# Hybrid encoder layer on one core: large element-wise passes of the DeltaNet phases taken off GpSimd

## The chip, the cores and the metric

One Trainium2 chip, one of its cores. The metric is the device time of one execution in microseconds (us); the time before is the median of three runs, 1222.3 us (1218.43 to 1222.52). Engines are named as the profile names them: PE is TensorE, PEld its weight loads, DVE VectorE, ACT ScalarE, POOL GpSimd, SP SyncE.

## What is computed

The reference is one encoder layer over two sequences of 512 and 256 tokens (768 in all, six tiles of 128), width 1024, in float32:

```python
h = rms_norm(x); proj = h @ w_in
att = window_attention(...)            # 8 query heads, 2 kv heads
dn = deltanet(...)                     # 4 heads of 128, both directions
x = x + rms_norm(concat([att, dn]) @ w_out)
x = x + rms_norm(cross_attention(rms_norm(x), mem, ...))   # 256 memory tokens
x = x + rms_norm(square(relu(rms_norm(x) @ w1)) @ w2)
```

The DeltaNet part needs, for each direction and head: a convolution over time of q, k and v; for each chunk a decay matrix `E`, a triangular matrix `L = -(k k') * E`, the inverse of `1 + L`, and the decayed attention product `(k q') * E`; then a scan over the chunks. The cross-attention needs keys and values of the normalised memory, `rms_norm(mem) @ xa_wkv`.

## The kernel before, in words

Float32 products are made on PE in a faster number format with a high and a low part: `hi` is the value rounded by ACT (line 107 for weights), `lo` the remainder `raw - hi` (line 108), and each product is three matmuls (hi hi, hi lo, lo hi). `Weights.emit` (line 93) does that for one unit of weights after another in a planned order: a transfer on SP's queue into one of two `raw` buffers (line 106), the copy on ACT (line 107), the subtraction on the engine that was passed in as `lo` (line 108). In the first half of the kernel that engine is GpSimd (lines 205 and 206); each kind of result tile, `whi` and `wlo`, has four buffers. From line 240 on (output projection, cross-attention, MLP) it is VectorE.

The order of work is that of `run` (line 192): projections and window attention; then `deltanet` for heads 0 and 1 while the convolution projections of heads 2 and 3 fill in (`proj_dn`, line 538); then `deltanet` for heads 2 and 3 while `fill` fills in (the z projections, the preparation of the memory, and its keys and values); then the output projection and the rest. `run(*gens)` only writes them one after the other. Which instruction really comes next on each engine is set at build time by a planner that takes program order as priority and its own costs for durations: DeltaNet's instructions stand first, and those of the later generators go where the planner sees an engine free. On the chip each engine then runs its own list strictly in that order.

`deltanet` has three parts. `prep` (line 676), for three groups of two tiles: two sets of four matmuls (lines 688 and 697), scaled out of PSUM by ACT into the single buffers `Gn` (line 693) and `Pa` (line 702); for each direction four DVE passes that form the exponent of the decay (line 708), its exponential on ACT (line 710), `L = Gn * E` on DVE (line 711) and `E = Pa * E` on GpSimd (line 712). `inverse` (line 714): DVE transposes (725, 726), a recurrence of 104 short DVE passes, `t = A * A` (line 734) and `A = A + t` (line 738), transposes again (741, 742), then small matmuls from line 764 on. The scan (`step`): matmuls with DVE, ACT and small GpSimd passes between them; each finished tile is normalised with two tiny GpSimd passes (883, 884) and a DVE pass (885).

`memory_prep` (line 368) takes four memory tiles of 128 x 1024: sum of squares on ACT (377), the scaling by the norm on GpSimd (379), eight transposes on PE into two PSUM banks (383), eight scaled copies out of PSUM on ACT (386), two rounded copies `hi` on ACT (388), and two subtractions `lo` on GpSimd (389).

Of the kernel before, what the change touches and what calls it, by code (L numbers as in the profile page):

```python
# [6 lines left out]
F32 = mybir.dt.float32  # L7
F32R = mybir.dt.float32r
AF = mybir.ActivationFunctionType
ALU = mybir.AluOpType  # L10
# [4 lines left out]
P = 128  # L15
# [42 lines left out]
def run(*gens):  # L58
    for _ in chain(*gens):
        pass  # L60
# [21 lines left out]
class Weights:  # L82
# [1 line left out]


    def __init__(self, nc, new, raw, lo):
        self.nc, self.new, self.raw, self.sub = nc, new, raw, lo.tensor_tensor
        self.q, self.done, self.n = [], {}, 0

    def plan(self, key, src, kk, n):  # L90
# [2 lines left out]
    def emit(self, upto):  # L93
        while self.n < min(upto, len(self.q)):
            key, src, kk, n = self.q[self.n]
            self.n += 1
            hi, lo = self.done[key] = self.new(kk, n)
            pool, size, bufs = self.raw
            rows = kk if callable(src) else size // n
            for k in range(0, kk, rows):  # L100
                c = slice(k, min(k + rows, kk))
                if callable(src):
                    raw = src()
                else:
                    raw = pool.tile([P, c.stop - k, n], F32, tag="raw", bufs=bufs, name="raw")
                    self.nc.sync.dma_start(raw, src[:, c])
                self.nc.scalar.activation(hi[:, c], raw, AF.Copy)  # L107
                self.sub(out=lo[:, c], in0=raw, in1=hi[:, c].bitcast(F32), op=ALU.subtract)  # L108

    def get(self, key, ahead=2):  # L110
        idx = next(i for i, u in enumerate(self.q) if u[0] == key)
# [4 lines left out]
class Kernel:  # L116
# [75 lines left out]
    def run(self):  # L192
        self.const, g_const = self.open("const")
        self.dram, g_dram = self.open("dram", space=DRAM)
        g_ps = self.banks(mm=2, tr=1, dnp=2, dns=1, wn=2)
        self.load_constants()
        self.scratch()


        big, g_big = self.open("big", side="left")  # L200
        self.hh, self.hl = (big.tile([P, 8, TOK], F32R, tag="big", bufs=2, name="h" + x) for x in "hl")
        cv, g_cv = self.open("conv", side="left")
        self.conv_buffers(cv)
        wp, g_w = self.open("wB", side="left")
        self.W = Weights(self.nc, lambda kk, n: [wp.tile([P, kk, n], F32R, tag=x, bufs=4, name="w" + x) for x in ("hi", "lo")],
                         (wp, 512, 2), self.nc.gpsimd)
        self.plan_b()
        self.plan_m()
        ap, g_ap = self.open("rope", side="left")
        k0, g_k0 = self.open("keep0", side="right")  # L210
        k1, g_k1 = self.open("keep1", side="right")
        pool, g = self.open("first", side="right")
        self.proj_first(pool, ap)
        self.close(g)
        at, g_at = self.open("att", side="right")
        keep0, keep1 = self.keep_tiles(k0), self.keep_tiles(k1)
        run(self.proj_att(ap, 1), self.proj_att(ap, 2))
        self.close(g_ap)
        run(merge((self.proj_dn(cv, 0, keep0, ("mm", "dnp")), 48), (self.window(at), 150)))
        self.close(g_at)  # L220
        dn, g_dn = self.open("dnw", side="right")
        self.dn_setup(dn)
        m0, g_m0 = self.open("mem0", side="right")
        run(self.deltanet(dn, 0, keep0), self.proj_dn(cv, 1, keep1, ("mm", "wn")))
        self.mem_gain = m0.tile([P, 8], F32, name="mgain")
        self.nc.sync.dma_start(self.mem_gain, self.a["mem_norm_g"][0].rearrange("(k p) -> p k", p=P))
        run(self.deltanet(dn, 1, keep1), self.fill(cv, m0, k0))

        group = []

        def unit(kk, n):

            if not group:
                i, unit.n = unit.n % 3 if unit.n < 6 else 0, unit.n + 1
                x = (big, big, wp)[i].tile([P, 2 if i == 2 else 3, 2, 1024], F32R, tag="big", bufs=1 if i == 2 else 2, name="w")
                group.extend((x[:, u, 0], x[:, u, 1]) for u in range(x.shape[1]))
            return [x.rearrange("p (k n) -> p k n", n=n) for x in group.pop(0)]

        unit.n = 0
        self.W = Weights(self.nc, unit, (wp, 512, 2), self.nc.vector)  # L240
        self.plan_c()
        self.W.emit(6)
        for g in (g_m0, g_dn, g_k1, g_k0, g_w, g_cv):
            self.close(g)
        self.close(g_ps)

        g_ps = self.banks(mm=3, tr=2, xa=2, up=1)
        self.hT = {}

        def h_tiles(s0, nt, side):  # L250
            pool, g = self.open(f"hx{s0}", side=side)
            self.hT[s0] = tuple(pool.tile([P, 8, nt * P], F32R, name=f"hx{s0}{n}") for n in "hl")
            return g

        g_h4 = h_tiles(*SEQS[1], "right")
        wp, g_w = self.open("wC", side="right")
        self.W.raw = wp, 1024, 2
        pool, g = self.open("tail", side="right")
        g_h0 = h_tiles(*SEQS[0], "left")
        up, g_up = self.open("up", side="left")  # L260
        xp, g_x = self.open("cross", side="left")
        self.tail(pool, xp)
        first = self.hidden(up)
        self.up(0, 4, first, "up", 0)
        for x in (g_x, g, g_w, g_ps):
            self.close(x)
        g_ps = self.banks(mm=4, y=4)
        wp, g_w = self.open("wD", side="right")
        self.W.raw, self.w2pool = (wp, 1024, 2), wp
        pool, g = self.open("mlp", side="left")  # L270
        self.mlp(pool, up, first)
        for x in (g, g_up, g_h0, g_w, g_h4, g_ps, g_big, g_dram, g_const):
            self.close(x)
# [94 lines left out]
    def memory_prep(self, m0, hh, hl):  # L368

        nc = self.nc  # L370
        for i in range(4):
            x = m0.tile([P, D], F32, tag="x", bufs=2, name="xm")
            src = self.a["mem_prompt"] if i < 2 else self.a["mem_sample"]
            nc.sync.dma_start(x, src[0, (i % 2) * P:(i % 2 + 1) * P, :])
            junk = m0.tile([P, D], mybir.dt.bfloat16, tag="junk", bufs=1, name="junk")
            ss = m0.tile([P, 1], F32, tag="ss", bufs=3, name="ss")
            nc.scalar.activation(junk, x, AF.Square, accum_out=ss)
            r = self.rsqrt(m0, ss, 1, 1.0 / D, EPS, "rs1")
            nc.gpsimd.tensor_scalar(x, x, r, 0.0, ALU.mult, ALU.add)
            for b in (0, 4):  # L380
                ps = self.ps(("tr", "mm")[b // 4], "tp")
                for j in range(4):
                    nc.tensor.transpose(ps[:, j * P:(j + 1) * P], x[:, (b + j) * P:(b + j + 1) * P], self.ident)
                h = x[:, b * P:(b + 4) * P].rearrange("p (k c) -> p k c", k=4)
                for j in range(4):
                    nc.scalar.activation(h[:, j], ps[:, j * P:(j + 1) * P], AF.Copy, scale=self.mem_gain[:, b + j:b + j + 1])
                hi, lo = hh[:, b:b + 4, i * P:(i + 1) * P], hl[b // 4][:, :, i * P:(i + 1) * P]
                nc.scalar.activation(hi, h, AF.Copy)
                nc.gpsimd.tensor_tensor(out=lo, in0=h, in1=hi.bitcast(F32), op=ALU.subtract)
            yield  # L390

    def memory_kv(self, pool, hh, hl):
# [283 lines left out]
    def prep(self, pool, half, keep, g, ts):  # L676

        nc = self.nc
        E, L = self.E[:, g], self.L[:, g]
# [19 lines left out]
        Pa = pool.tile([P, 4, P], F32, tag="S4", bufs=1, name="Pa")  # L699
# [3 lines left out]
        for d in range(2):  # L703
            ds = slice(4 * d, 4 * d + 4)
            for tt, t in enumerate(ts):
                for h in range(2):
                    e, col = 4 * d + 2 * tt + h, 4 * d + 2 * half + h
                    nc.vector.scalar_tensor_tensor(out=E[:, e], in0=E[:, e], scalar=self.cole[:, t, col:col + 1],
                                                   in1=self.emask[:, d], op0=ALU.subtract, op1=ALU.min)
            nc.scalar.activation(E[:, ds], E[:, ds], AF.Exp)  # L710
            nc.vector.tensor_tensor(out=L[:, ds], in0=Gn, in1=E[:, ds], op=ALU.mult)
            nc.gpsimd.tensor_tensor(out=E[:, ds], in0=Pa, in1=E[:, ds], op=ALU.mult)

    def inverse(self, pool):

# [606 lines left out]
```

## Time and profile before

| what | before |
|---|---|
| median of three runs | 1222.3 us |
| time of the profiled execution | 1220.31 us |
| its span | 1218.5 us |
| mean granted clock of PE | 0.965 |
| busy PE / DVE / ACT / POOL | 1117.1 / 706.6 / 530.5 / 438.7 us |

All times in the rows further down are from the start of the span. Busy time of PE counts a matmul at whatever clock was granted. The stretches that matter for the change are 227 to 300 us (`prep` and `inverse` of heads 0 and 1), 300 to 340 (their scan), 340 to 370 (`prep` of heads 2 and 3), 370 to 412 (their `inverse`), 412 to 470 (their scan) and 470 to 530 (the last values of the memory and the first tiles of the output projection).

### The profile page before, as it was taken

The page shows a single profiled execution, that of the slowest core. Times are in us where ns is not written, and L with a number is a line of the kernel's source. Part 1 is how long each engine was busy: PE and PEld are TensorE (multiplying, and loading weights), DVE is VectorE, ACT ScalarE, POOL GpSimd, SP SyncE. Part 2 cuts the span into 40 slices and gives each one's busy share as a digit, 9 for nine tenths or more (in the row PEclk, how much of TensorE's full clock was granted, in tenths as well). Part 3 has the DMA queues.
Part 4 walks back from the last instruction along what each step waited for, and adds up shares of the span by engine and source line. Part 5 has one row for each costly group of instructions (what it writes and reads, how often), then busy time and mean ns, then how long its engine had stood idle before and what let it go on. Part 6 is the DMA issues. An engine that isn't in the chain of part 4 may idle for free.

```text
span 1218.5 us, 17803 instructions
## 1 busy us (share of the span) xinstructions
PE 1117.1 (92%) x6800; PEld 955.7 (78%) x6800; DVE 706.6 (58%) x1183; ACT 530.5 (44%) x1123; POOL 438.7 (36%) x475
## 2 busy tenths in 40 slices
PE   5998999877987698889898989999999999999995
PEld 5887888766876586678787778888888888888884
DVE  5313564799569741446635646365658565658656
ACT  5336766664466333433534534432333323333322
POOL 5354321453147323011101137353526253527461
PEclk9999999988798899999999999999999999999998
DMA  6355321311123116842722142122212222212115
GB/s 198 97 173 162 96 62 26 90 42 44 28 70 109 45 48 203 268 135 87 236 76 70 70 138 84 55 70 70 87 52 69 70 70 69 87 52 61 45 52 172
DMA packets 108703, 113.81 MB, mean 93 GB/s; under 512 B 10079, under 2 KB 81867, under 8 KB 108619
## 3 DMA queue, kind: packets, MB, share of 16 engines
q1 hardware_dynamic: 100971, 99.55, 27.0%
q10 hardware_dynamic: 7648, 13.13, 2.9%
q8 instruction: 53, 0.87, 0.3%
q14 instruction: 31, 0.25, 0.1%
HBM read 91.27 MB, written 21.39 MB: 92 GB/s over the span
## 4 chain that ended last, share of the span: by engine, by line
PE 47%; DMA 4%; issue 3%; DVE 3%; POOL 3%; ACT 2%; ACTq 0%; POOLq 0%; DVEq 0%; SPq 0%
PE up L1194 7%; PE up L1195 7%; PE up L1196 7%; PE y L189 5%; PE y L187 5%; PE y L188 5%; DMA raw<-in_w_out 2%; PE mm L189 2%; PE mm L187 2%; PE mm L188 2%; POOL y L1256 1%; DVE w L108 1%; DMA raw<-in_xa_wo 1%; ACT w L107 1%; PE xa L1155 1%
## 5 line engine op out<-in xcount | busy, mean ns | idle before, releaser
L1199 POOL TENSOR_TENSOR hid<-hid 128x256 f32<-128x256 f32 (+1 forms) x64 | 61.1, 955 | 221.9 <-ACT hid L1198 213.1
L108 POOL TENSOR_TENSOR wlo<-raw,whi 128x512 fp32r<-128x512 f32 (+1 forms) x61 | 83.6, 1374 | 137.2 <-ACT whi L107 98.6
L189 PE MATMUL y<-w,hl 128*128 128x512 f32 x318 | 123.8, 389 | 0.5 <-DVE hl L183 0.5
L188 PE MATMUL y<-w,hh 128*128 128x512 f32 x318 | 123.7, 389 | 0.0
L187 PE MATMUL y<-w,hh 128*128 128x512 f32 x318 | 123.7, 389 | 0.0
L1238 DVE TENSOR_TENSOR y<-y,y 128x512 f32<-128x512 f32 x72 | 48.9, 683 | 107.1 <-PE y L189 107.1
L1198 ACT ACTIVATE hid<-up 128x256 f32<-128x256 f32 (+1 forms) x64 | 31.3, 488 | 177.2 <-PE up L1196 177.2
L1194 PE MATMUL up<-hx0h,w 128*128 128x512 f32 x256 | 100.0, 391 | 1.6 <-DVE hx0l L183 1.6
L108 DVE TENSOR_TENSOR w<-raw,w 128x1024 fp32r<-128x1024 f32 (+1 forms) x58 | 78.9, 1366 | 37.6 <-ACT w L107 37.6
L1195 PE MATMUL up<-hx0l,w 128*128 128x512 f32 x256 | 100.0, 390 | 0.0
L1196 PE MATMUL up<-hx0h,w 128*128 128x512 f32 x256 | 99.6, 389 | 0.0
L996 POOL TENSOR_TENSOR quad<-quad 128x1024 f32<-128x1024 f32 x28 | 77.4, 2764 | 33.2 <-DVE w L108 20.6
L108 DVE TENSOR_TENSOR w<-quad,w 128x1024 fp32r<-128x1024 f32 x49 | 72.6, 1492 | 12.5 <-ACT w L107 12.5
L1194 PE MATMUL up<-hx4h,w 128*128 128x256 f32 x256 | 72.2, 282 | 4.3 <-ACT hid L1198 4.3
L107 ACT ACTIVATE w<-raw 128x1024 fp32r<-128x1024 f32 (+1 forms) x58 | 55.5, 963 | 38.5 <-DMA raw<-in_w_out 14.1
L1195 PE MATMUL up<-hx4l,w 128*128 128x256 f32 x256 | 71.7, 280 | 0.1
L1196 PE MATMUL up<-hx4h,w 128*128 128x256 f32 x256 | 71.4, 279 | 0.0
L189 PEld LDWEIGHTS y<-w,hl 128*128 128x128 f32 x318 | 59.7, 188 | 13.3 <-DVE hl L183 0.9
L188 PEld LDWEIGHTS y<-w,hh 128*128 128x128 f32 x318 | 59.7, 188 | 12.4
L187 PEld LDWEIGHTS y<-w,hh 128*128 128x128 f32 x318 | 59.7, 188 | 12.4
L182 ACT ACTIVATE hh<-hid 128x768 fp32r<-128x768 f32 x37 | 31.4, 848 | 81.9 <-PE y L188 64.0
L107 ACT ACTIVATE whi<-raw 128x512 fp32r<-128x512 f32 (+1 forms) x61 | 37.9, 625 | 50.3 <-DMA raw<-in_xa_wkv 12.3
(373 smaller groups left out, 3152.4 us busy)
## 6 DMA issues: line engine op xcount, KB each, us to landing
raw<-in_mlp_w SPq DMA_DIRECT2D x36, 512.0 KB, 4.5
quad<-in_mlp_w SPq DMA_DIRECT2D x28, 512.0 KB, 4.6
raw<-in_w_in SPq DMA_DIRECT2D x44, 256.0 KB, 2.9
d_x<-x ACTq DMA_DIRECT2D x12, 512.0 KB, 2.6
x<-d_x SPq DMA_DIRECT2D x12, 512.0 KB, 3.8
x<-in_x_prompt SPq DMA_DIRECT2D x8, 512.0 KB, 3.7
raw<-in_xa_wkv SPq DMA_DIRECT2D x16, 256.0 KB, 2.9
d_att<-parts SPq DMA_DIRECT2D x12, 256.0 KB, 2.0
```

The source lines that it names most:

```text
L107: self.nc.scalar.activation(hi[:, c], raw, AF.Copy)
L108: self.sub(out=lo[:, c], in0=raw, in1=hi[:, c].bitcast(F32), op=ALU.subtract)
L182: nc.scalar.activation(hi, src, AF.Copy)
L187: nc.tensor.matmul(ps, lh, rh, start=first, stop=False)
L188: nc.tensor.matmul(ps, lh, rl, start=False, stop=False)
L189: nc.tensor.matmul(ps, ll, rh, start=False, stop=last)
L996: nc.gpsimd.tensor_tensor(out=out, in0=x, in1=y, op=ALU.subtract)
L1194: nc.tensor.matmul(ps, wh[:, k], hh[:, k], start=k == 0, stop=False)
L1195: nc.tensor.matmul(ps, wh[:, k], hl[:, k], start=False, stop=False)
L1196: nc.tensor.matmul(ps, wl[:, k], hh[:, k], start=False, stop=k == 7)
L1199: nc.gpsimd.tensor_tensor(out=r, in0=r, in1=r, op=ALU.mult)
L1238: nc.vector.tensor_tensor(out=y, in0=y, in1=ps, op=ALU.add)
```

## The change

Four moves. The low parts of weights: those of the attention projections, of the small gate projection and of DeltaNet's heads 0 and 1 stay on GpSimd; those of heads 2 and 3 (12 units), of z (8) and of the memory's keys and values (16) go to VectorE. The decayed attention product (line 712) goes to VectorE. The scaling of the memory by its norm (line 379) goes to ScalarE. The memory's high parts are rounded straight out of PSUM on ScalarE, which drops the eight copies of line 388, and its low parts are made by VectorE out of PSUM in 32 passes of 128 x 128 in place of GpSimd's eight of 128 x 512. All else is the same text.

```diff
-        self.nc, self.new, self.raw, self.sub = nc, new, raw, lo.tensor_tensor
+        self.nc, self.new, self.raw = nc, new, raw
+        self.sub = lambda key: lo(key).tensor_tensor
...
-                self.sub(out=lo[:, c], in0=raw, in1=hi[:, c].bitcast(F32), op=ALU.subtract)
+                self.sub(key)(out=lo[:, c], in0=raw, in1=hi[:, c].bitcast(F32), op=ALU.subtract)
...
-                         (wp, 512, 2), self.nc.gpsimd)
+                         (wp, 512, 2), lambda key: self.nc.gpsimd if key[0] in ("att", "ba") or key[0] == "dn" and key[2] < 2 else self.nc.vector)
...
-        self.W = Weights(self.nc, unit, (wp, 512, 2), self.nc.vector)
+        self.W = Weights(self.nc, unit, (wp, 512, 2), lambda key: self.nc.vector)
...
-            nc.gpsimd.tensor_scalar(x, x, r, 0.0, ALU.mult, ALU.add)
+            nc.scalar.activation(x, x, AF.Copy, scale=r)
...
-                h = x[:, b * P:(b + 4) * P].rearrange("p (k c) -> p k c", k=4)
+                hi, lo = hh[:, b:b + 4, i * P:(i + 1) * P], hl[b // 4][:, :, i * P:(i + 1) * P]
                 for j in range(4):
-                    nc.scalar.activation(h[:, j], ps[:, j * P:(j + 1) * P], AF.Copy, scale=self.mem_gain[:, b + j:b + j + 1])
-                hi, lo = hh[:, b:b + 4, i * P:(i + 1) * P], hl[b // 4][:, :, i * P:(i + 1) * P]
-                nc.scalar.activation(hi, h, AF.Copy)
-                nc.gpsimd.tensor_tensor(out=lo, in0=h, in1=hi.bitcast(F32), op=ALU.subtract)
+                    g = self.mem_gain[:, b + j:b + j + 1]
+                    nc.scalar.activation(hi[:, j], ps[:, j * P:(j + 1) * P], AF.Copy, scale=g)
+                    nc.vector.scalar_tensor_tensor(out=lo[:, j], in0=ps[:, j * P:(j + 1) * P], scalar=g,
+                                                   in1=hi[:, j].bitcast(F32), op0=ALU.mult, op1=ALU.subtract)
...
-            nc.gpsimd.tensor_tensor(out=E[:, ds], in0=Pa, in1=E[:, ds], op=ALU.mult)
+            nc.vector.tensor_tensor(out=E[:, ds], in0=Pa, in1=E[:, ds], op=ALU.mult)
```

## Rows read from the trace of the kernel before

**Rows 1.** Busy time of each engine, share of the span, instructions (the page's first part).

```profile
PE 1117.1 (92%) x6800; PEld 955.7 (78%) x6800; DVE 706.6 (58%) x1183; ACT 530.5 (44%) x1123; POOL 438.7 (36%) x475
```

**Rows 2.** Stretches: PE, PEld, DVE, ACT, POOL busy us; granted clock, DMA share, GB/s.

```profile
227.00:300.00 73.00, 57.56 (x396) 49.45 (x395) 70.96 (x169) 40.66 (x106) 33.69 (x28) 0.88 0.21 58
...
370.00:412.00 42.00, 24.30 (x135) 20.54 (x136) 41.24 (x113) 21.13 (x48) 22.69 (x20) 0.80 0.30 96
```

**Rows 3.** PE's waits from 150 to 560 us: total, times, longest.

```profile
PE tr L567 <- DVE room L562: 12.1, 2, 6.3
PE dnp L764 <- DVE C L741: 10.3, 1, 10.3
...
PE mm L504 <- ACT z L515: 6.3, 1, 6.3
PE dnp L688 <- ACT Gn L693: 2.4, 2, 2.2
...
PE dnp L697 <- ACT Pa L702: 2.1, 3, 1.0
```

**Rows 4.** Groups of POOL by form, 190 to 530 us: busy, mean ns, idle before.

```profile
L108 POOL TENSOR_TENSOR wlo<-raw,whi 128x512 fp32r<-128x512 f32 x35 | 48.7, 1392 | 104.9 <-ACT whi L107 77.0 <-PE tp L383 11.4 <-PE wS L936 6.0
L712 POOL TENSOR_TENSOR E<-Pa,E 128x512 f32<-128x512 f32 x12 | 17.4, 1465 | 12.4 <-ACT Pa L702 4.6 <-DVE L L711 4.1 <-DMA E<-d_gc 1.9
```

**Rows 5.** POOL's passes of line 108 alone, by stretch.

```profile
227.00:300.00 73.00, 17.61 (x11) 0.88 0.21 58
...
370.00:412.00 42.00, 7.84 (x6) 0.80 0.30 96
```

**Rows 6.** POOL's passes of line 389 alone, by stretch.

```profile
370.00:412.00 42.00, 8.00 (x6) 0.80 0.30 96
```

**Rows 7.** Groups of DVE by form, 190 to 530 us.

```profile
L824 DVE SCALAR_TENSOR_TENSOR C<-dns,negc,room 128x128 f32<-128x128 f32 x32 | 9.2, 344 | 9.8 <-PE dns L821 9.4 <-issue 0.3
L108 DVE TENSOR_TENSOR w<-raw,w 128x512 fp32r<-128x512 f32 x12 | 8.3, 692 | 18.8 <-ACT w L107 18.8
```

**Rows 8.** Lines 708 and 711 on their own: minimum/median/maximum ns, first and last start.

```profile
L708 DVE SCALAR_TENSOR_TENSOR E<-E,cole,emask x48: 337/346/1391, 227.2 to 358.4; 128x128 f32<-128x128 f32 x48
L711 DVE TENSOR_TENSOR L<-Gn,E x12: 675/682/1785, 230.6 to 369.6; 128x512 f32<-128x512 f32 x12
```

**Rows 9.** Groups of DVE by form, 227 to 247 us.

```profile
L708 DVE SCALAR_TENSOR_TENSOR E<-E,cole,emask 128x128 f32<-128x128 f32 x24 | 12.8, 600 | 5.4 <-DMA E<-d_gc 5.4
```

**Rows 10.** DVE's recurrence alone (lines 734, 738: passes on `t`), by stretch.

```profile
253.00:294.00 41.00, 26.13 (x104) 0.84 0.18 45
375.00:401.30 26.30, 25.72 (x54) 0.87 0.37 116
```

**Rows 11.** DVE in order of time in the second inverse: start, length of the merged piece.

```profile
390.46 2.67 DVE L734 TENSOR_TENSOR t<-A 128x136 f32<-128x136 f32 x2
393.06 0.47 DVE L738 TENSOR_TENSOR A<-A,t 128x136 f32<-128x136 f32 x2
```

**Rows 12.** Groups of ACT by form, 190 to 530 us.

```profile
L388 ACT ACTIVATE hm<-xm 128x512 fp32r<-128x512 f32 x8 | 5.0, 636 | 0.0
...
L377 ACT ACTIVATE junk<-xm 128x1024 bf16<-128x1024 f32 x2 | 2.1, 1050 | 0.0
```

**Rows 13.** The chain of waits, 440 to 560 us: start, length, piece.

```profile
466.40 1.30 POOL wlo L108
467.94 0.70 POOL oss L884
...
475.21 1.28 POOL wlo L108
```

**Rows 14.** ACT's waits from 227 to 300 us.

```profile
ACT whi L107 <- PE mm L505: 3.5, 1, 3.5
ACT whi L107 <- issue: 3.5, 2, 2.8
```

**Rows 15.** ACT's waits from 370 to 412 us.

```profile
ACT whi L107 <- DMA raw<-in_xa_wkv: 5.6, 1, 5.6
```

## The prediction

> **What bounds the kernel now.** I read the page's busy times first, then the stretches, then what PE waits for in them. PE is busy for 92% of the span [rows 1], so the time is PE's work plus the places where PE stands or runs at the lower clock. The stretches show where those are [rows 2]. From 227 to 300 us PE works 57.6 of 73 us and from 370 to 412 only 24.3 of 42, and in both DVE is the full engine (71.0 and 41.2 us). The granted clock in them is 0.88 and 0.80, a mix of 2.4 and 1.2 GHz, after PE had stood. So in these stretches DVE's list and the order of PE's list set the pace, not PE's work. PE's waits name the rest [rows 3]: 12.1 us in two waits for the convolution's last pass on DVE (line 562), 10.3 us in one for the end of the second inverse, 6.3 us for ACT's copy of z, and 4.5 us for `Gn` and `Pa` in `prep`. GpSimd itself is hardly named. Its passes matter in two other ways: DVE passes are longer while a large GpSimd pass runs, and ACT and the transfers wait for GpSimd's slow ends.
>
> **What GpSimd's passes cost DVE.** In the second inverse a pair of recurrence passes takes 0.47 us, and a like pair beside GpSimd's subtractions 2.67 us [rows 11]. Pairs follow each other every 0.39 us, so one pass alone is worth some 0.2 us. The first inverse's 104 passes took 26.1 us, that is 5.3 over 104 x 0.2; in the second, 54 passes took 25.7 us, and at some 0.24 for these, which hold the longest shapes, 13.0 would do: 12.7 over [rows 10]. Line 708's 24 passes in the first `prep` took 600 ns each [rows 9] against a least 337 [rows 8]: 24 x 0.263 = 6.3 us. So DVE can get back 6.3 + 5.3 = 11.6 us in the first stretch and 12.7 in the second inverse. As a rule this is in the Trainium skill, SBUF — State Buffer, section "SBUF: two separate sides": a GpSimd pass and a DVE pass with two SBUF inputs exclude each other, and the loser blocks fully. The trace agrees with the 2.67 beside the 0.47.
>
> **What DVE gets instead.** A low part costs GpSimd 1.39 us [rows 4] and DVE 0.69 [rows 7]. The decayed product costs 1.47 on GpSimd [rows 4]; on DVE the same shape with the same operands costs 0.68 undisturbed [rows 8]. In the first stretch stand 11 low parts [rows 5] and 6 of the 12 products: 11 x 0.69 + 6 x 0.68 = 11.7 us. In the second inverse stand 6 low parts [rows 5] and 6 of the memory's eight subtractions [rows 6]; these become 6 x 4 passes of 128 x 128 out of PSUM, and the nearest such pass (line 824) takes 0.344 [rows 7]: 6 x 0.69 + 24 x 0.344 = 12.4 us. So on DVE both stretches come out even: 11.6 returned for 11.7 added, 12.7 for 12.4. I count DVE's list in itself as **nothing**. Bounds: if none of the passes is placed inside the bound parts, it is 12 us less in each; if nothing is returned, 12 more in each.
>
> **What is left that shortens the time.**
> (a) `Pa` has one buffer, and PE and ACT wait for it while GpSimd takes 1.47 us per direction. At 0.68 a group of two directions is done 1.6 us sooner. Of the 4.5 us that PE waits for `Gn` and `Pa` I take 2 off.
> (b) PE's two waits of together 12.1 us for the convolution stay, as DVE's sum in that stretch stays: 0.
> (c) z. Its copies on ACT stand behind `prep`'s chain and behind two of the eight rounded copies of the memory, 0.64 us each [rows 12]. Those copies are gone: 1.3 us; with the shorter chain of (a) I take 3 of the 6.3 off. The norm scaling that ACT takes over (four passes of 128 x 1024, the nearest row 1.05 us [rows 12]) adds 4.2 us in place of 8 x 0.64 = 5.1, so ACT is not fuller.
> (d) The end of the second inverse. The last two of the memory's subtractions end shortly before 400 us and the first product with the memory's keys cannot start earlier; on PE's list the inverse's first matmul stands before it, and PE stands for 10.3 us. When the memory's low parts come from DVE right behind ACT's copy, these products can be placed before the inverse ends, and there are enough of them to fill the whole wait. That depends on the planner's order, which the trace cannot show: between 0 and 10.3, I take 5.
> (e) The tail. The chain that ends last passes three of GpSimd's low parts, 1.3 us each, between 466 and 477 us, and the small normalisation pass on GpSimd stands in line behind the first of them [rows 13]. With 0.69 each that is 3 x 0.6 = 1.8, and 1.2 for the pass that need not queue: 3 us. What is late next there is the transfer that the freed buffer starts, which then starts earlier too.
> Sum: 2 + 0 + 3 + 5 + 3 = 13 us. The profiled execution took 1220.3 us, 2.0 below the median of the runs shown; 1222.3 - 13 gives **1209 us**. Covers: GpSimd's remaining small passes are hidden by PE's work; the attention stretch before 227 us keeps its order but for the first two memory scalings, which ACT has room for. From 530 us on the instructions are the same.
>
> **The page's rule against this change.** Splitting a pass multiplies a fixed part: from the rows, 32 passes of 0.344 are 11.0 us where eight of 0.69 would be 5.5. The Trainium skill, VectorE: DVE Perf Modes, section on the TRN2 errata, says the same (a fixed cost per instruction, so tiles of 512 or more are wanted), and by its 120 + 128 cycles out of PSUM, an estimate, the 32 passes would be 8.3 us. By that the sum would be 2 us better in the second inverse; the row decides.
>
> **Rivals.**
> *DVE waits for weights (slower).* DVE runs its list in order. A low part on it waits for ACT's copy, and that waits for a raw transfer, 5.6 us inside the second inverse [rows 15], or for a buffer or ACT's own line, 3.5 and 3.5 us inside the first stretch [rows 14]. On GpSimd such waits cost nothing: it stood 104.9 us before line 108 [rows 4]. If the planner puts these low parts among the recurrence passes and takes the transfers for shorter than they are, DVE stands for 12.6 us in the stretches where it is the full engine; then each inverse ends later, (c) and (d) do not come, and (a) and (e) remain: 1222.3 + 12.6 - 5 = **1230 us**. It decides from the point where DVE's waits in its own list pass the 5 us of (a) and (e). For it: 71.0 of 73 us on DVE [rows 2], so nothing can be caught up. Against: the low parts come far down in program order, so the planner has reason to place them where DVE is free, after the inverses.
> *An even trade (no change).* DVE gives as it takes, and PE's order is as before: (c) and (d) stay. Then only (a) and (e) count: 1222.3 - 5 = **1217 us**.
> *The whole lock comes back (much faster).* GpSimd's large passes in the two stretches are 17.6 + 6 x 1.47 = 26.4 and 7.8 + 8.0 = 15.8 us. If DVE, or the passes behind it, had been held for all of that and not the 11.6 and 12.7 that I read, 18 us more are free, and with them the waits of 12.1, 10.3 and 6.3 go, beside (a) and (e): 12.1 + 10.3 + 6.3 + 5 = 34, **1188 us**. The rule of the Trainium skill named above, taken in full, would do that. Against: the measured excess is what it is.
>
> **How the numbers follow.** Forecast 0.50, even trade 0.20, DVE waits for weights 0.18, the whole lock 0.08, and 0.04 for a planner's order that moves something else, split evenly. About 0.5% (6.1 us) can be told from no change, so faster is below 1216.2 and slower above 1228.4. The forecast's own range, with (a), (c), (d) between nothing and their whole waits, is 1198 to 1217; a few of its cases and the even trade fall within 0.5%. Faster 0.60, same 0.22, slower 0.18. Signs differ, so the range reaches from **1190**, short of the whole lock, to **1229**, short of the full price of the waits.
>
> **What would show it.** Right: DVE's line 708 near 0.34 us and the second recurrence near 21 us in all; PE's wait at line 764 below 6 us; no wait for GpSimd's line 108 in the last chain; ACT's wait for line 712 gone. Wrong: DVE waiting for line 107's copy inside the two inverses, by more than 8 us together; or PE's waits at lines 567 and 764 as long as before, which would be the even trade.

## The result, and the profile after

The changed kernel took 1212.8 us (median of four runs, 1210.7 to 1215.1) where the kernel before took 1222.4: a ratio of 0.9941 with a 95% interval of 0.9916 to 0.9966. Measured a second time (the last experiment below) it was 0.9954 [0.9928, 0.998]. So it is faster by about half a per cent, and the forecast of 1209 is 3.8 us off. The profiled execution took 1215.1 us with a span of 1213.3, against a span of 1218.5 before. Lines up to 85 keep their numbers; behind that all lines of the new kernel are one higher, but for the rewritten lines of `memory_prep`, where 388 is ACT's rounded copy and 389 the low part on DVE.

The page's first part, busy time by engine. Beside [rows 1] POOL has 83 us less; DVE and ACT differ by less than 2 us, and PE has 2.9 us more for the same 6800 matmuls:

```profile
PE 1120.0 (92%) x6800; PEld 958.7 (79%) x6800; DVE 708.1 (58%) x1263; ACT 529.4 (44%) x1119; POOL 355.5 (29%) x415
```

The stretches, in the columns of [rows 2]:

```profile
227.00:300.00 73.00, 56.36 (x549) 47.59 (x548) 68.95 (x191) 43.01 (x108) 10.94 (x11) 0.88 0.19 47
...
353.00:366.00 13.00, 0.81 (x5) 0.81 (x5) 11.92 (x31) 11.34 (x27) 0.75 (x2) 0.63 0.08 20
...
400.00:410.00 10.00, 10.00 (x61) 7.68 (x60) 3.53 (x10) 2.53 (x8) 0.00 (x0) 0.50 0.01 2
410.00:420.00 10.00, 10.00 (x75) 9.21 (x73) 3.25 (x8) 2.23 (x6) 0.00 (x0) 0.61 0.09 26
```

DVE is still the full engine from 227 to 300 us. Two new things stand in the second half: from 353 to 366 us PE does almost nothing, and from 400 to 420 it works without a gap at a granted clock of 0.50 and 0.61, that is mostly at the lower of its two levels. In the kernel before, PE's work behind the end of the second inverse, from 412 to 480 us, had 0.97.

What PE waits for from 150 to 560 us, the answer to [rows 3]:

```profile
PE mm L505 <- DVE wlo L109: 15.2, 2, 8.5
PE tp L384 <- DVE hm L389: 12.2, 1, 12.2
PE tr L408 <- ACT kvo L402: 4.9, 2, 3.4
...
PE dnp L765 <- DVE C L742: 0.6, 1, 0.6
PE tr L568 <- ACT room L571: 0.5, 1, 0.5
PE mm L505 <- ACT z L516: 0.4, 1, 0.4
PE dnp L698 <- ACT Pa L703: 0.4, 1, 0.4
...
PE tr L568 <- DVE y L563: 0.4, 1, 0.4
```

Every wait of [rows 3] has nearly gone, and two others stand in their place. Both are for low parts on DVE: the weights' (`wlo`, line 109) and the memory's (`hm`, line 389). Over the whole span PE stands (span less busy time) 93.3 us where it stood 101.4. Of these 8.1 us its longer busy time takes 2.9 back, and the 5.2 us between the spans are left.

DVE's passes on `t`, by stretch, the answer to [rows 10]. Together they returned 6.6 and 14.1 us (the second recurrence took 33.4 us before: 25.72 for the 54 passes shown and 7.67 for the other 50):

```profile
250.00:284.00 34.00, 19.48 (x104) 0.81 0.15 39
...
361.00:386.00 25.00, 19.29 (x104) 0.82 0.25 82
```

Where the gain went shows in two marks. One is the start of DVE's last transpose of each inverse; the other is ACT's copy of the memory's values, the last of which ends the work that the second inverse holds up. First the kernel before (count, least/median/most ns, first and last start), then the kernel after:

```profile
L742 DVE STREAM_TRANSPOSE C<-A x2: 1204/1212/1221, 295.3 to 410.9; 128x1024 f32<-128x1024 f32 x2
...
L409 ACT ACTIVATE kvv<-tr x4: 581/598/600, 476.4 to 501.5; 128x512 f32<-128x512 f32 x4
```

```profile
L743 DVE STREAM_TRANSPOSE C<-A x2: 1203/1204/1204, 286.3 to 389.2; 128x1024 f32<-128x1024 f32 x2
...
L410 ACT ACTIVATE kvv<-tr x4: 579/597/599, 474.9 to 496.3; 128x512 f32<-128x512 f32 x4
```

The first inverse ends 9.0 us sooner and the second 21.7. At the last of the memory's values only 5.2 us are left, and 5.2 is also the difference of the spans. So the change is decided by about 500 us: it wins 21.7 us up to the end of the second inverse and gives 16.5 of them back before 497.

It gives them back at the memory's low parts. DVE's order of time around the start of the second inverse, and then PE's:

```profile
356.77 3.32 DVE L726 STREAM_TRANSPOSE C<-L 32x384 f32<-32x384 f32 x4
360.12 0.35 DVE L389 SCALAR_TENSOR_TENSOR hm<-tp,mgain,hm 128x128 fp32r<-128x128 f32 x1
360.39 1.24 DVE L727 STREAM_TRANSPOSE A<-C 128x1024 f32<-128x1024 f32 x1
361.55 0.31 DVE L389 SCALAR_TENSOR_TENSOR hmr<-tp,mgain,hm 128x128 fp32r<-128x128 f32 x1
...
363.96 0.35 DVE L389 SCALAR_TENSOR_TENSOR hm<-tp,mgain,hm 128x128 fp32r<-128x128 f32 x1 [0.41 <-ACT hm L388]
...
364.79 0.34 DVE L389 SCALAR_TENSOR_TENSOR hm<-tp,mgain,hm 128x128 fp32r<-128x128 f32 x1
```

```profile
351.79 1.16 PE L698 MATMUL dnp<-room 128*128 128x128 f32 x8
365.19 1.11 PE L384 MATMUL tp<-ident,xm 128*128 128x128 f32 x4 [12.25 <-DVE hm L389]
```

PE's next transposes of the memory need a PSUM bank that is free only when the fourth low part out of it has run. These passes stand on DVE's list behind `prep`'s passes, behind 3.3 and 1.2 us of transposes, and then between passes of the recurrence; the fourth starts at 364.8 and PE at 365.2. Before, ACT alone emptied these banks, and GpSimd subtracted out of SBUF. The last low parts run only at 411.8 and 415.8 us, long after the inverse:

```profile
L389 DVE SCALAR_TENSOR_TENSOR hmr<-tp,mgain,hm x16: 310/344/351, 347.7 to 411.8; 128x128 fp32r<-128x128 f32 x16
L389 DVE SCALAR_TENSOR_TENSOR hm<-tp,mgain,hm x16: 338/344/351, 360.1 to 415.8; 128x128 fp32r<-128x128 f32 x16
```

### The profile page after: what moved, and what is told of

The parts are those of the page before. It is cut to its first block, busy times and chain, and to the rows that moved or that the text cites. A ratio compares the mean times of both kernels' runs of the same rounds, so it can differ in the third digit from the quotient of the medians.

```text
span 1213.3 us, 17783 instructions
## 1 busy us (share of the span) xinstructions
PE 1120.0 (92%) x6800; PEld 958.7 (79%) x6800; DVE 708.1 (58%) x1263; ACT 529.4 (44%) x1119; POOL 355.5 (29%) x415
## 4 chain that ended last, share of the span: by engine, by line
PE 42%; issue 3%; POOL 2%; DVE 2%; DMA 1%; ACT 1%; POOLq 0%; DVEq 0%; ACTq 0%
PE up L1195 7%; PE up L1196 7%; PE up L1197 7%; PE y L189 5%; PE y L188 5%; PE y L190 5%; POOL y L1257 1%; DMA raw<-in_xa_wo 1%; PE xa L1156 1%; PE xa L1137 1%; PE mm L1121 1%; PE mm L1120 1%; PE mm L1119 1%; POOL rs L153 1%; PE mm L188 0%
## 5 line engine op out<-in xcount | busy, mean ns | idle before, releaser
L190 PEld LDWEIGHTS y<-w,hl 128*128 128x128 f32 x318 | 59.7, 188 | 13.3 <-DVE hl L184 0.9
L184 DVE TENSOR_TENSOR hl<-hid,hh 128x768 fp32r<-128x768 f32 x37 | 43.0, 1162 | 24.8 <-ACT hh L183 24.6
L1195 PEld LDWEIGHTS up<-hx0h,w 128*128 128x128 f32 x256 | 48.1, 188 | 10.4 <-DVE hx0l L184 1.2
```

Of the source, the lines that this page charges most:

```text
L184: nc.vector.tensor_tensor(out=lo, in0=src, in1=hi.bitcast(F32), op=ALU.subtract)
L190: nc.tensor.matmul(ps, ll, rh, start=False, stop=last)
L1195: nc.tensor.matmul(ps, wh[:, k], hh[:, k], start=k == 0, stop=False)
```

## The experiments

Three kernels make one part of the change alone, each on the kernel before. Then parts of the change are taken back or moved, GpSimd work is put in, and the memory's low parts are made in two other ways. All ratios are to the kernel before, run beside it on the same chip. There it took 1218.0 us beside the three single parts and the kernel with heads 2 and 3 back on GpSimd, 1219.3 beside the last two, and 1216.9 beside the others; absolute times are to be read against these. The planner orders the instructions of every kernel anew, so each edit is measured together with the order that it brings.

**The product alone.**

```diff
-            nc.gpsimd.tensor_tensor(out=E[:, ds], in0=Pa, in1=E[:, ds], op=ALU.mult)
+            nc.vector.tensor_tensor(out=E[:, ds], in0=Pa, in1=E[:, ds], op=ALU.mult)
```

> Before, with the decayed product (line 712) alone moved to VectorE. Theory A (GpSimd's large passes lengthen VectorE's two-input passes, and the change gives that time back): line 708's 24 passes in the first prep fall from 600 ns to under 400, that stretch ends some 4 us sooner, the second prep some 2; both recurrences stay as long as before (26 and 33 us). Time 1216 to 1220. Theory B (the passes do not disturb each other; only the planner's new order counts): line 708 stays near 600 ns, time 1222 within 2.

Measured: 0.9959 [0.9936, 0.9982], some 5 us, as expected. DVE's line 708 in the first `prep` falls from 600 ns [rows 9] to 382, but the recurrences, beside which no product runs, keep most of theirs, 24.9 and 32.8 us for 26.1 and 33.4. PE's waits from 150 to 560 us:

```profile
PE dnp L764 <- DVE C L741: 13.4, 1, 13.4
PE tr L567 <- DVE room L562: 11.1, 4, 6.0
```

So the product shortens `prep` and nothing else: the two large waits of before stay.

**The weights' low parts alone** (the selection by key, with the rest of `Weights` as in the change).

```diff
-                         (wp, 512, 2), self.nc.gpsimd)
+                         (wp, 512, 2), lambda key: self.nc.gpsimd if key[0] in ("att", "ba") or key[0] == "dn" and key[2] < 2 else self.nc.vector)
```

> Before, with the low parts of 36 weight units alone moved to VectorE. Theory A: the first recurrence falls from 26 to about 20 us, the second from 33 to about 26 (the memory's passes on GpSimd still stand beside it); TensorE waits for low parts in VectorE's list, some 10 to 15 us in the first stretch, so the sum is small: 1214 to 1222. Theory B: recurrences as before; time set by the order alone, 1222 or more.

Measured: 0.9896 [0.9853, 0.9939], 1203.2 us. By its median this part alone gains more than the whole change (the intervals overlap a little). It is also more than the 1214 to 1222 us expected of it from a before of 1222, of which the ratio makes 1210: the waits for low parts are 6.3 and 1.4 us, not 10 to 15. The recurrences take 19.5 and 25.2 us, and the last copy of the memory's values starts at 479.0 us, 17 us before that of the change. PE's waits:

```profile
PE tr L408 <- ACT kvo L402: 6.8, 2, 4.7
PE mm L190 <- DVE wlo L109: 6.3, 1, 6.3
PE tr L568 <- DVE room L563: 5.6, 1, 5.6
```

**The memory alone** (`memory_prep` as in the change).

```diff
-            nc.gpsimd.tensor_scalar(x, x, r, 0.0, ALU.mult, ALU.add)
+            nc.scalar.activation(x, x, AF.Copy, scale=r)
...
-                    nc.scalar.activation(h[:, j], ps[:, j * P:(j + 1) * P], AF.Copy, scale=self.mem_gain[:, b + j:b + j + 1])
...
-                nc.scalar.activation(hi, h, AF.Copy)
-                nc.gpsimd.tensor_tensor(out=lo, in0=h, in1=hi.bitcast(F32), op=ALU.subtract)
...
+                    nc.scalar.activation(hi[:, j], ps[:, j * P:(j + 1) * P], AF.Copy, scale=g)
+                    nc.vector.scalar_tensor_tensor(out=lo[:, j], in0=ps[:, j * P:(j + 1) * P], scalar=g,
+                                                   in1=hi[:, j].bitcast(F32), op0=ALU.mult, op1=ALU.subtract)
```

> Before, with the memory's scaling and high and low parts alone changed (ScalarE, VectorE). Theory A: the second recurrence falls from 33 to about 25 us, the first stays near 26; TensorE's transposes of the memory wait for VectorE's low parts to free the bank, 5 to 12 us, so about even: 1216 to 1224. Theory B: second recurrence stays at 33 us.

Measured: 1.0088 [1.0054, 1.0122], slower by about 11 us, although the second recurrence falls from 33.4 to 23.6 us. PE's waits:

```profile
PE tr L567 <- DVE room L562: 13.4, 2, 7.8
PE tp L383 <- DVE hm L388: 8.7, 1, 8.7
...
PE dns L829 <- DVE C L824: 5.7, 3, 4.7
```

The wait for the memory's bank is there with this part alone. These rows do not show the loss itself: of the six executions, 1218 to 1231 us, the profiled one is the shortest, PE stands in it 102.3 us against 101.4 before, and its mean granted clock is 0.969 where the other five had 0.959 to 0.964. The three parts make -0.41, -1.04 and +0.88%, together -0.57%; the change measured -0.59 and -0.46%. It is about their sum: two gains and a loss.

**The change without the memory's part** (`memory_prep` as before).

```diff
-            nc.scalar.activation(x, x, AF.Copy, scale=r)
+            nc.gpsimd.tensor_scalar(x, x, r, 0.0, ALU.mult, ALU.add)
...
+                    nc.scalar.activation(h[:, j], ps[:, j * P:(j + 1) * P], AF.Copy, scale=self.mem_gain[:, b + j:b + j + 1])
...
-                    nc.scalar.activation(hi[:, j], ps[:, j * P:(j + 1) * P], AF.Copy, scale=g)
-                    nc.vector.scalar_tensor_tensor(out=lo[:, j], in0=ps[:, j * P:(j + 1) * P], scalar=g,
-                                                   in1=hi[:, j].bitcast(F32), op0=ALU.mult, op1=ALU.subtract)
+                nc.scalar.activation(hi, h, AF.Copy)
+                nc.gpsimd.tensor_tensor(out=lo, in0=h, in1=hi.bitcast(F32), op=ALU.subtract)
```

> The changed kernel with the memory's preparation as before (scaling and low parts on GpSimd, eight rounded copies on ScalarE). If the parts add up (product -0.4%, weights -1.0%, memory +0.9% when done alone), this is about 0.986 of before, 1201 us where before is 1218. Theory: TensorE's 12.2 us wait for the memory's low parts at the bank goes; the second recurrence grows from 19.3 to about 25 us, as in the run with the weights alone. Rival (the parts overlap, the sum being set by VectorE's fullness in the inverses): between the weights alone and the change, 0.990 to 0.994.

Measured: 0.9896 [0.9867, 0.9925], 1203.7 us. The loss goes when the part is taken back. But it is no better than the weights alone, so the product's 0.4% does not show on top (both intervals are as wide as that). The added-up 0.986 lies just outside the interval and the rival's 0.990 inside it. The second recurrence takes 27.5 us. PE's waits, in which no bank of the memory stands for DVE:

```profile
PE mm L505 <- DVE wlo L109: 14.5, 3, 9.3
PE wn L505 <- DVE wlo L109: 5.6, 1, 5.6
```

**Heads 2 and 3 back on GpSimd.** The low parts of these heads' weights are those that PE waited 15.2 us for.

```diff
-... or key[0] == "dn" and key[2] < 2 else ...
+... or key[0] == "dn" else ...
```

> The changed kernel, with the 12 low parts of heads 2 and 3 back on GpSimd. Theory A with the cost side (TensorE's 15.2 us of waits for low parts in VectorE's list are what the change gives back): those waits fall under 3 us, the first recurrence grows from 19.5 to about 25 us, and the net is a gain of 5 or more on the changed kernel: 1203 to 1208. Rival (those waits stand where TensorE would wait for the convolution on VectorE anyway): no gain or a loss, 1212 to 1218.

Measured: 1.0000 [0.9977, 1.0023]. The waits for `wlo` are gone, and the ratio is worse than the change's. The recurrences stay short, 20.5 and 19.3 us; the 25 expected of GpSimd's passes beside the first did not come. In this order, though, at most four of GpSimd's low parts stand beside it, where seven stood in the kernel before. PE's waits:

```profile
PE dnp L765 <- DVE C L742: 8.8, 1, 8.8
PE tp L384 <- DVE hm L389: 7.8, 1, 7.8
PE tr L568 <- DVE room L563: 5.7, 2, 3.6
```

**The same low parts earlier on DVE** (the planner's high priority for them).

```diff
...
-                self.sub(key)(out=lo[:, c], in0=raw, in1=hi[:, c].bitcast(F32), op=ALU.subtract)
+                with self.soon(key):
+                    self.sub(key)(out=lo[:, c], in0=raw, in1=hi[:, c].bitcast(F32), op=ALU.subtract)
...
+        self.W.soon = lambda key: self.tc.high_priority() if key[0] == "dn" and key[2] > 1 else nullcontext()
...
```

> The changed kernel, with the low parts of heads 2 and 3 put ahead in the planner's priority, so that they stand on VectorE's list before the DeltaNet passes and not among the recurrence. Theory (TensorE's two waits of 15.2 us for these low parts are a cost of the order): the waits fall under 4 us, time 5 to 10 us below the changed kernel. Rival (TensorE waits in the same stretch for something else of VectorE's): waits for line 563's convolution pass or the inverse's end take their place, time within 3 us of the changed kernel.

Measured: 1.0007 [0.9988, 1.0025]. Again no wait for `wlo`, and again no gain. PE's waits (this kernel's lines are four higher behind the diff):

```profile
PE dnp L769 <- DVE C L746: 12.7, 1, 12.7
PE tp L388 <- DVE hm L393: 7.8, 1, 7.8
```

The inverses end at 293.3 and 400.7 us in place of 286.3 and 389.2. So in these two orders the 15.2 us are not won, by order or by engine: with the low parts sooner, PE waits at the inverse's end. What is short there is DVE's time.

**GpSimd's passes put back, needless ones.** Eight passes of 128 x 512 at the start of each recurrence, on a buffer that nothing reads before it is rewritten; the outputs do not use them.

```diff
         nc.vector.transpose(A, C1)
+        lk = C2[:, 0:16]
+        nc.gpsimd.tensor_tensor(out=lk, in0=C1[:, 0:16], in1=C1[:, 16:32], op=ALU.subtract)
+        for j in range(7):
+            nc.gpsimd.tensor_tensor(out=lk, in0=lk, in1=lk, op=ALU.subtract)
```

> The changed kernel with eight needless GpSimd passes of 128 x 512 (subtractions on a buffer that is free then) during each recurrence; their result is not used and the planner's order on the other engines is nearly the same. If GpSimd's passes hold up VectorE's two-input passes: each recurrence grows from 19.4 us by 6 to 10 us, the GpSimd passes themselves take more than 1.28 us each where they meet it, and the time grows by 5 to 15 us. If not: recurrences within 1 us, time within 3 us of the changed kernel.

Measured: 1.0069 [1.0051, 1.0087]. DVE's passes on `t`, by stretch; in the change they take 19.5 and 19.3 us:

```profile
220.00:320.00 100.00, 24.48 (x104) 0.86 0.19 52
320.00:440.00 120.00, 23.84 (x104) 0.84 0.18 54
```

The same 104 passes grow by 5.0 and 4.5 us, about 0.6 for each needless pass; 6 to 10 were expected. The cause that the prediction read out of the pairs of 2.67 and 0.47 us [rows 11] is thus shown, at a smaller size. By the ratios the kernel is some 14 us slower than the change; in its trace PE waits 15.4 us for a low part of the memory (line 389) alone. The planner's order of the other engines was not wholly the same, so only the recurrences are read from it, not the total.

**The memory's low parts out of SBUF, whole.** As the change, but ACT first copies the scaled memory to SBUF, where it rounds it and DVE subtracts in eight passes of 128 x 512.

```diff
...
+                    nc.scalar.activation(h[:, j], ps[:, j * P:(j + 1) * P], AF.Copy, scale=self.mem_gain[:, b + j:b + j + 1])
...
-                    nc.scalar.activation(hi[:, j], ps[:, j * P:(j + 1) * P], AF.Copy, scale=g)
-                    nc.vector.scalar_tensor_tensor(out=lo[:, j], in0=ps[:, j * P:(j + 1) * P], scalar=g,
-                                                   in1=hi[:, j].bitcast(F32), op0=ALU.mult, op1=ALU.subtract)
+                nc.scalar.activation(hi, h, AF.Copy)
+                nc.vector.tensor_tensor(out=lo, in0=h, in1=hi.bitcast(F32), op=ALU.subtract)
```

> The changed kernel with the memory's low parts on VectorE, but as eight passes of 128 x 512 out of SBUF (the scaled copy is written to SBUF on ScalarE first, as before, and its eight rounded copies are back), so the PSUM bank is free after ScalarE's copies. If the bank held for VectorE is the memory part's cost: TensorE's 12.2 us wait goes, and the time is near that of the kernel with the memory as before, within 3 us. If VectorE's fullness is: time near the changed kernel.

Measured: 0.9818 [0.98, 0.9837], 1194.4 us, by clear intervals below the change and below the kernel with the memory as before; neither theory expected that. The stretches, DVE's passes, and the two marks:

```profile
353.00:366.00 13.00, 11.27 (x69) 9.88 (x69) 12.49 (x26) 11.60 (x29) 0.00 (x0) 1.00 0.22 62
...
400.00:410.00 10.00, 10.00 (x114) 8.43 (x114) 4.77 (x10) 3.06 (x6) 0.00 (x0) 1.00 0.35 107
```

```profile
L390 DVE TENSOR_TENSOR hmr<-xm,hm x4: 681/683/689, 346.8 to 385.9; 128x512 fp32r<-128x512 f32 x4
...
L743 DVE STREAM_TRANSPOSE C<-A x2: 1208/1214/1219, 286.0 to 388.5; 128x1024 f32<-128x1024 f32 x2
...
L410 ACT ACTIVATE kvv<-tr x4: 581/597/598, 453.4 to 476.8; 128x512 f32<-128x512 f32 x4
```

The inverses end where they end in the change, 286.0 and 388.5. But PE works 11.3 of the 13 us in which it stood there, the low parts are all done by 386.6, and the memory's values start their last copy at 476.8 in place of 496.3. The 19.5 us between these two are the 21 us between the spans (1213.3 and 1192.2), but for 1.6. The wait for `wlo` is as long as in the change (15.1 us), so it is not that wait which holds the change back.

**The same, cut into four.** Out of SBUF as above, but each low part in four passes of 128 x 128 (the diff is to the whole passes).

```diff
-                nc.vector.tensor_tensor(out=lo, in0=h, in1=hi.bitcast(F32), op=ALU.subtract)
+                for j in range(4):
+                    nc.vector.tensor_tensor(out=lo[:, j], in0=h[:, j], in1=hi[:, j].bitcast(F32), op=ALU.subtract)
```

> As the run with the memory's low parts in whole passes on VectorE, but each pass of 128 x 512 cut into four of 128 x 128, still out of SBUF: as many VectorE passes as in the changed kernel (32), but no PSUM bank waits for them. If the bank held for VectorE is what costs: TensorE's transposes of the memory wait for ScalarE alone, time within 4 us of the whole passes (ratio to before 0.980 to 0.986). If the number of VectorE passes is what costs: ratio 0.990 or more, near the changed kernel.

**The change again**, on the same chip.

> The changed kernel itself once more, beside the others on one chip, to have its ratio more closely: between 0.992 and 0.997 of before if the first measurement holds.

Measured: cut into four 0.9896 [0.9864, 0.9928], the change 0.9954 [0.9928, 0.998]. First the rows of the cut kernel, a stretch, a wait of PE and DVE's passes; then PE's waits in the change:

```profile
400.00:410.00 10.00, 10.00 (x63) 7.06 (x62) 3.84 (x8) 2.03 (x4) 0.00 (x0) 0.50 0.17 48
```

```profile
PE mm L189 <- DVE hm L391: 3.3, 1, 3.3
```

```profile
L391 DVE TENSOR_TENSOR hmr<-xm,hm x16: 282/283/293, 348.9 to 396.6; 128x128 fp32r<-128x128 f32 x16
```

```profile
PE mm L505 <- DVE wlo L109: 15.0, 2, 8.3
PE tp L384 <- DVE hm L389: 12.2, 1, 12.2
```

In the repeat the change has the same two waits to 0.2 us. The cut kernel has no wait for a bank, yet it regains only 0.6 of the 1.4 points between the change and the whole passes. The other 0.8 lies between 32 passes and eight: 32 x 0.283 = 9.1 us of DVE for 8 x 0.683 = 5.5, the last of them 11 us later, a wait of 3.3 us for them, and the lower clock from 400 us on. Neither cause alone explains the loss: the way through the bank makes 0.6 points and the splitting 0.8, each known to some 0.4. (The two kernels out of SBUF were not timed together, but each against the kernel before.)

The two cost PE in different ways. The page's first part, of the whole passes and of the cut ones:

```profile
PE 1105.7 (93%) x6800; PEld 945.8 (79%) x6800; DVE 704.9 (59%) x1239; ACT 533.4 (45%) x1127; POOL 359.1 (30%) x415
```

```profile
PE 1118.7 (93%) x6800; PEld 955.7 (79%) x6800; DVE 706.7 (59%) x1263; ACT 534.2 (44%) x1127; POOL 353.9 (29%) x415
```

| profiled execution | span | PE busy | PE stands | busy times granted clock |
|---|---|---|---|---|
| before | 1218.5 us | 1117.1 us | 101.4 us | 1089 us |
| the change | 1213.3 us | 1120.0 us | 93.3 us | 1090 us |
| out of SBUF, cut in four | 1207.2 us | 1118.7 us | 88.5 us | 1090 us |
| out of SBUF, whole | 1192.2 us | 1105.7 us | 86.5 us | 1092 us |

The last column, PE's busy time multiplied by the granted clock microsecond by microsecond, is the same work in all four, so the busy times differ by the clock. From the change to the cut kernel the span falls by 6.1 us, and 4.8 of these are standing. From the cut kernel to the whole passes it falls by 15.0 us, and 13.0 of these are clock. All executions bear that out: the five with whole passes had a mean clock of 0.979 to 0.981, the six cut ones 0.969 to 0.972.

## Why the prediction was right, and which step was wrong

The time and its sign came as forecast, and so did the signs of the terms but for one. That the sum came so near is luck, as two errors cancel: the waits that went were larger than forecast, and new ones came.

- **(a) `Gn` and `Pa`**: 2 us of 4.5 forecast; 4.5 became 0.4. Mechanism right, gain larger. ACT's wait for line 712, 4.1 us from 150 to 560 us, is no longer among its waits, as forecast.
- **(b) the convolution's waits**: forecast to stay. 12.1 us became 0.9, and 15.2 us for the weights' low parts stand in their place. The net, 4 us worse, is near the forecast nothing, but it came by another way: PE waits for a place on DVE's list, the mirror of the first rival, in which DVE was to wait for the weights. DVE itself waits only 0.2 us for line 108's copy between 340 and 400 us, and not at all from 227 to 290, so that rival's own sign did not come. The experiments with heads 2 and 3 show no way to do better: without these waits DVE ends the inverse later.
- **(c) z**: 3 of 6.3 forecast; 6.3 became 0.4.
- **(d) the end of the second inverse**: 5 of 10.3 forecast; 10.3 became 0.6, near the upper bound.
- **(e) the tail**: 3 forecast. PE's waits from 470 to 530 us fell from 13.3 to 9.3 us, and no low part of GpSimd is left in the chain that ends last, which now starts at 577 us.
- **"I count DVE's list in itself as nothing"** was mis-sized. The recurrences returned 20.7 us where 18.0 were forecast (the second took 19.3 us, near the 21 named as a sign), and line 708 came down to the 0.34 forecast (0.346; [rows 9]: 600). But of the 11 weights' low parts counted into the first stretch only 8 lie there (6 up to 287 us), and 18 of the memory's 32 passes, not 24, run before the second inverse ends. So the inverses ended 9.0 and 21.7 us sooner. The moved work was counted where GpSimd had done it; the planner put part of it elsewhere.
- **The step that failed** is the memory's subtractions, "these become 6 x 4 passes of 128 x 128 out of PSUM", costed only as DVE time. Its duration was exact (0.344). What was left out is what each pass holds: the bank that ACT had emptied by itself is now free only when a busy engine, working in order, comes to it. That is the wait of 12.2 us, and with the low parts out of SBUF, still cut in four, it goes and 0.6 points come back. The other 0.8 points are the splitting, which the prediction had only as DVE time too. Alone, the memory's part, that was to help, loses 0.88%; how these two share that loss was not measured.

Added up over PE's waits: (a) to (e) gave 4.1 + 11.2 + 5.9 + 9.7 + 4.0 = 34.9 us, about the 34 of the third rival, in which all these waits go; the two new waits took 27.4. The 7.5 left are near the 8.1 us by which all of PE's standing fell, of which the clock took 2.9 back. So that rival's list of waits was right and its price was not, because DVE had no room to serve both.

The even trade (1217) fails by the same rows: z and the end of the inverse did not stay. The forecast's own range has a slip: with (a), (c) and (d) at nothing, (e) alone gives 1219, not 1217. The splitting, which the prediction counted as 11.0 us of DVE's time for 5.5, bore more weight than its time on DVE. The Trainium skill, VectorE: DVE Perf Modes, section on the TRN2 errata, wants tiles of 512 or more. The trace agrees with the rule's direction, 9.1 us for 5.5; but the cut and the whole passes differ by 0.8%, some 9 us, more than the 3.6 us between these sums, and most of it is the lower clock.

Why the clock fell is left open. It was 0.50 from about 397.5 to 417.5 us in the change and from 395.5 to 419.5 in the cut kernel, with PE working almost without a gap, and 1.00 there in the kernel with whole passes; 20 us at half the clock cost about 10, an estimate. PE had stood shortly before both falls: 1.7 us for ACT's `Z` (line 768) in the change, in the row below (1.7 us in its repeat too, with the fall again 2 us later), and the 3.3 us for the memory's low part, up to 395.6 us, in the cut kernel. With whole passes its longest wait from 386 to 400 us is 0.9 us.

```profile
395.83 1.10 PE L772 MATMUL dnp<-Z,L 32*32 32x32 f32 x45 [1.70 <-ACT Z L768]
```

In the change the clock had also fallen inside the wait of 12.2 us, and stood at 0.50 from about 356.5 to 370 us. No run sets the clock apart from the waits before it, so that the short waits caused the second fall is likely and not shown.

## What to carry to other kernels

Moving large passes off GpSimd paid here, where VectorE's passes with two SBUF inputs set the pace, but a moved pass must be costed with what it holds as well as with its duration: here it was best to let the engine that had room copy a PSUM bank out at once, and to do the rest out of SBUF in few whole passes. Make each part of such a change alone, since a sum of half a per cent hid two gains and a loss of 0.9. And when a wait on a full engine is removed by order, look for it at that engine's next deadline before counting it as won. Beside the waits, compare PE's busy time for the same matmuls: most of what the splitting cost stood there and not in a wait.

## What the runs showed of the hardware that was not expected

- A GpSimd pass of 128 x 512 beside the recurrence cost DVE's passes about 0.6 us, though each took GpSimd longer: the needless passes of the loop took 1040 to 1750 ns, median 1076. The Trainium skill, SBUF — State Buffer, section "SBUF: two separate sides", has the loser blocked fully; by that rule, an estimate that takes each pass to block for all of its measured time, it would be at least 8 x 1.04 = 8.3 us in each recurrence. 5.0 and 4.5 were measured, and 6.6 for the seven low parts beside the first recurrence of the kernel before, which took GpSimd 1.3 us or more each.
- A DVE pass of 128 x 128 took 344 ns with one input out of PSUM (scaled and subtracted, line 389) and 283 with both out of SBUF (subtracted only); one of 128 x 512 out of SBUF took 683. So four small passes out of SBUF cost 1.66 times one large.
- In the traces of all eleven kernels PE's busy time multiplied by the granted clock is 1087 to 1092 us, while the busy time itself runs from 1106 to 1120 us: between kernels with the same matmuls, nearly all of the difference in busy time was clock.
